# Dividing the filling down unit of a seven-product pair into two halves by blocks of tokens

## The chip, the core and the metric

One core of one Trainium2 chip runs the whole program, in one launch. The metric is the time of that launch on the device in microseconds (us), the median of three runs; smaller is better.

## The reference, cut to what matters

Ten stages follow each other on a matrix x of 256 tokens by 1024 features, in fp32. Six of them are feed-forward blocks and are all that the change touches:

```
def swiglu(h, w_gate, w_up, w_down):
    return (jax.nn.silu(h @ w_gate) * (h @ w_up)) @ w_down
```

Two of these have 2816 hidden features (22 tiles of 128), four have 4096 (32 tiles; gate and up are then the two halves of one matrix). The other four stages (two mixers of the first model, two hybrid mixers of the second) hold attention, retention and a delta rule.

## The kernel before, in words

**Split operands.** Every fp32 weight is split into two parts of type fp32r: `hi`, a rounded copy, and `lo`, the rest (`prep`, L139). A product of two split matrices is three matmuls, hi·hi, hi·lo and lo·hi (`mm3`, L270). A *unit* is one weight block of up to 128 x 2048 numbers. It is loaded in two halves of 128 x 1024 by SyncE's DMA queue (L151), ScalarE (ACT) casts each to `hi` (L154), VectorE (DVE) subtracts to get `lo` (L155). `hi` and `lo` have four buffers each. `pump` (L193) prepares units until four are ready ahead of the last one used (AHEAD), so a unit that has been used up gives its buffer to the one four places later.

**A feed-forward block** (`ffn`, L614) goes over chunks of 256 hidden features, C = 11 or 16 of them. An ordinary chunk (`chunk`, L653) multiplies x by a gate unit and an up unit and makes h = silu(gate)·up. Each chunk has also a *down* unit, which multiplies its h by the chunk's rows of w_down and adds into four PSUM accumulators y (`emit_down`, L755): for each block b of 128 tokens 12 matmuls of 512 columns, 24 in all. The down units of a chunk are emitted after the next chunk's gate and up products (`downs`, L771).

**The seven-product pair** (`quad`, L704) takes two chunks at once, c and c+1, at c = 3 and 7 (C = 11) or 3, 7 and 11 (C = 16): 2·2 + 4·3 = 16 pairs in the program. By a scheme in the manner of Strassen's it needs seven products of 128-token blocks where eight would do it plainly; each is 12 matmuls of 512 columns. Their names and order are 11, T1, T2, T3, 21, T4, 22. The weights of T1 to T4 are differences of weight blocks, made by DVE in fp32 before the split (`combine`, L160); the sums of x are made once for each block (`sums`, L677), at its start. Three PSUM banks p, q, r take the products: 11 and 21 go to p, T2, T3 and T4 to q (T3 and T4 are added onto what is there, start=False), T1 and 22 to r.

DVE reads the banks between the products: `add(u2, p1, q)` after T2 (L725; called **the u2 add** here), `add(u3, p1, q)` after T3 (L728; **the u3 add**), `add(u3, u3, r)`, then `add(g1, p1, q)` after T4, and so on; all of these show as line L279 with `s<-s,work`, 128x512. T3 adds into q, so it can't start before the u2 add has read q; T4 likewise waits for the u3 add. Between T2 and T3 stands `fill()` (L726): one open down unit, both blocks, 24 matmuls. Between T3 and T4 stands the product 21, 12 matmuls.

**What sets the order.** TensorE (PE) runs in the order of the program text (`manual_schedule`, L780). The other engines' instructions are put in order when the program is compiled: the tile scheduler goes through the work in time order and takes on each engine, of what is ready, what stands first in the program text. On the chip each engine then runs its own list in that order. The preparation that a product's `pump` asks for stands in the text right behind the product, and so ahead of the addition that reads the product's bank.

Of the kernel before, what the change touches and what calls it, by code (L numbers as in the profile page):

```python
# [98 lines left out]
def kslab(w, k0, k1, c0, c1):  # L99
    return w[128 * k0:128 * k1, c0:c1].reshape(k1 - k0, 128, c1 - c0).transpose(1, 0, 2)  # L100
# [18 lines left out]
class Net:  # L119
# [494 lines left out]
    def ffn(self, nt, gate, up, down, nxt):  # L614
# [4 lines left out]
        hs = {}  # L619
# [33 lines left out]
        def chunk(c):  # L653
            ps = []
            for src in (gate, up):
                def fn(inp, src=src):
                    w, a, z = cols(src, c)(inp)
                    return kslab(w, 0, 8, a, z)
                u = self.unit((8, 256), fn)
                p = self.tile(512)  # L660
                for j in range(2):
                    self.fold(p, j, self.x_tile(u, j))
                    if late and (src is up or j == 1):
                        late.pop(0)()
                ps.append(p)
                if src is gate:
                    sg = self.tile(512)
                    self.act(sg, p, AF.Silu)
                    self.pump()
            h = self.tile(2, 256)  # L670
            self.mul(h.rearrange("p a b -> p (a b)"), sg, ps[1])
            hp = self.pair(2)
            self.split(hp[0], hp[1], h)
            self.pump()
            return hp
# [28 lines left out]
        def quad(c, fill):  # L704

            def cut(src, k, inp):
                return kslab(src[0](inp), 4 * k, 4 * k + 4, src[1] + 256 * c, src[1] + 256 * c + 512)
            data = {"11": (gate, 0), "T1": (up, 0), "T2": (up, 1), "21": (gate, 1)}

            def product(ps, mode, l, start):  # L710
                fn = (lambda inp: cut(*data[mode], inp)) if mode in data else None
                w = self.unit((4, 512), fn, mode)
                for k in range(4):
                    self.mm3(ps, (l[0][:, k], l[1][:, k]), (w[0][:, k], w[1][:, k]), start and k == 0, k == 3, True)
                self.pump()

            def x(b, k):
                return tuple(t[:, 4 * k:4 * k + 4, 128 * b:128 * b + 128] for t in self.xT)
            p, q, r = (self.work() for _ in range(3))
            p1, u2, u3, sg, g1 = (self.tile(512) for _ in range(5))  # L720
            product(p, "11", x(0, 0), True)
            self.cp(p1, p)
            product(r, "T1", S[1], True)
            product(q, "T2", S[2], True)
            self.add(u2, p1, q)  # L725
            fill()  # L726
            product(q, "T3", S[3], False)
            self.add(u3, p1, q)  # L728
            self.add(u3, u3, r)
            product(p, "21", x(0, 1), False)  # L730
            self.act(sg, p, AF.Silu)
            product(q, "T4", x(1, 1), False)
            self.add(g1, p1, q)
            self.act(g1, g1, AF.Silu)
            self.mul(u3, u3, g1)
            product(r, "22", S[4], False)
            self.add(u2, u2, r)
            self.mul(u2, u2, sg)
            hq = {}

            def back(b, h):
                def fn():
                    hq[b] = self.tile(4, 128, dt=F32R), self.tile(4, 128, dt=F32R)
                    ps = self.work()
                    for k in range(4):
                        self.tr(ps[:, 128 * k:128 * k + 128], h[:, 128 * k:128 * k + 128])
                    self.split(hq[b][0], hq[b][1], ps.rearrange("p (k t) -> p k t", k=4))
                return fn
            late.extend([back(1, u3), back(0, u2)])
            return [lambda j, b, i=i: tuple(t[:, 2 * i + j] for t in hq[b]) for i in range(2)]  # L750

        def unit_down(c):
            return self.unit((2, 1024), lambda inp: kslab(down(inp), 2 * c, 2 * c + 2, 0, 1024))

        def emit_down(c, b, w, js=range(2), ns=range(2)):  # L755
            for j in js:
                for n in ns:
                    self.mm3(y[b][n], hs[c](j, b),
                             (w[0][:, j, 512 * n:512 * n + 512], w[1][:, j, 512 * n:512 * n + 512]),
                             c == 0 and j == 0, c == C - 1 and j == 1)  # L760

        def plain(hp):
            return lambda j, b: tuple(t[:, j, 128 * b:128 * b + 128] for t in hp)
# [5 lines left out]
        open_ = list(range(HEAD))  # L769

        def downs(n=1000):  # L771
            while open_ and n:
                n -= 1
                e = open_.pop(0)
                w = unit_down(e)
                for b in range(2):
                    emit_down(e, b, w)
                self.pump()
        c = HEAD
        with self.tc.manual_schedule(engines={mybir.EngineType.PE}):  # L780
            while c < C:
                if c in QUADS[C]:
                    hs[c], hs[c + 1] = quad(c, lambda: downs(1))
                    new = [c, c + 1]
                else:
                    hs[c] = plain(chunk(c))
                    new = [c]
                c += len(new)
                if c == C - 1:
                    self.load_next(nxt)  # L790
                downs()
                open_ += [e for e in new if e < C - TAIL]
# [1018 lines left out]
```

## Time and profile before

| | |
|---|---|
| median of 3 runs | 2328.01 us (2327.23 to 2329.88) |
| the profiled execution's own time | 2330.61 us |
| its span | 2328.5 us |
| PE busy | 2279.9 us (98%) |
| DVE busy | 1817.3 us (78%) |
| ACT busy | 1312.9 us (56%) |
| moved by DMA | 419.08 MB, mean 180 GB/s |

The profiled execution's own time is its span and some 2.1 us around it. Times in rows are microseconds from the start of the span. Matmuls overlap: one of 512 columns shows a length of 0.39 us but the next starts 0.23 us later, so lengths of waits are read from starts.

### The profile page before, as it was taken

The page shows a single profiled execution, that of the slowest core. Times are in us where ns is not written, and L with a number is a line of the kernel's source. Part 1 is how long each engine was busy: PE and PEld are TensorE (multiplying, and loading weights), DVE is VectorE, ACT ScalarE, POOL GpSimd, SP SyncE. Part 2 cuts the span into 40 slices and gives each one's busy share as a digit, 9 for nine tenths or more (in the row PEclk, how much of TensorE's full clock was granted, in tenths as well). Part 3 has the DMA queues.
Part 4 walks back from the last instruction along what each step waited for, and adds up shares of the span by engine and source line. Part 5 has one row for each costly group of instructions (what it writes and reads, how often), then busy time and mean ns, then how long its engine had stood idle before and what let it go on. Part 6 is the DMA issues. An engine that isn't in the chain of part 4 may idle for free.

```text
span 2328.5 us, 31780 instructions
## 1 busy us (share of the span) xinstructions
PE 2279.9 (98%) x12094; PEld 1946.6 (84%) x12094; DVE 1817.3 (78%) x2424; ACT 1312.9 (56%) x1950; POOL 93.9 (4%) x149
## 2 busy tenths in 40 slices
PE   8999999999999999999999999999999999999998
PEld 7788888887887888878998888878888889988887
DVE  6688776679859886887678888698877876778885
ACT  6655554455646555764555556465556654555663
POOL 4200000000000000000000000000000000000000
PEclk9999999999999999999999999999999999999999
DMA  7365555565366535543265663565555533576532
GB/s 242 132 226 186 188 197 173 191 237 200 125 229 210 190 132 204 179 156 123 91 213 213 217 217 136 192 227 187 167 178 197 172 105 101 174 259 208 204 130 91
DMA packets 120552, 419.08 MB, mean 180 GB/s; under 512 B 14408, under 2 KB 17224, under 8 KB 120400
## 3 DMA queue, kind: packets, MB, share of 16 engines
q1 hardware_dynamic: 120112, 416.53, 52.7%
q8 instruction: 95, 1.56, 0.3%
q10 hardware_dynamic: 288, 0.52, 0.1%
q14 instruction: 57, 0.47, 0.1%
HBM read 415.95 MB, written 1.05 MB: 179 GB/s over the span
## 4 chain that ended last, share of the span: by engine, by line
PE 45%; DVE 6%; DMA 2%; issue 1%; POOL 1%; ACT 0%; SPq 0%; POOLq 0%; DVEq 0%; ACTq 0%
PE acc L268 24%; PE work L268 20%; DVE lo L155 3%; DVE s L279 2%; PE work L276 2%; DMA raw<-in_w 1%; DMA s<-in_w 1%; POOL c L311 0%; ACT hi L154 0%; SPq L166 0%; POOL c L312 0%; DVE s L291 0%; DVE c L1460 0%; DVE x L279 0%; DVE s L552 0%
## 5 line engine op out<-in xcount | busy, mean ns | idle before, releaser
L155 DVE TENSOR_TENSOR lo<-raw,hi 128x1024 fp32r<-128x1024 f32 (+3 forms) x644 | 755.0, 1204 | 196.0 <-ACT hi L154 186.4
L154 ACT CAST hi<-raw 128x1024 fp32r<-128x1024 f32 (+3 forms) x644 | 642.3, 1035 | 311.3 <-PE work L268 87.5
L268 PE MATMUL acc<-hi,s 128*128 128x512 f32 (+1 forms) x1736 | 550.3, 391 | 0.0
L268 PEld LDWEIGHTS acc<-hi,s 128*128 128x128 f32 x1736 | 325.9, 188 | 66.3 <-ACT s L301 0.6
L268 PE MATMUL work<-x,hi 128*128 128x512 f32 x1472 | 371.8, 394 | 5.9 <-DVE s L279 5.9
L268 PE MATMUL work<-hi,x 128*128 128x512 f32 x1024 | 328.8, 392 | 10.9 <-DVE s L279 10.3
L268 PE MATMUL acc<-lo,s 128*128 128x512 f32 (+1 forms) x868 | 338.0, 389 | 0.0
L279 DVE TENSOR_TENSOR s<-s,s 128x512 f32<-128x512 f32 (+3 forms) x378 | 310.9, 849 | 31.9 <-ACT s L301 21.6
L154 ACT CAST hi<-s 128x1024 fp32r<-128x1024 f32 x224 | 228.9, 1051 | 166.8 <-DVE s L279 72.1
L268 PEld LDWEIGHTS work<-x,hi 128*128 128x128 f32 x1472 | 266.7, 188 | 57.7 <-DVE s L279 8.0
L155 DVE TENSOR_TENSOR lo<-s,hi 128x1024 fp32r<-128x1024 f32 x224 | 266.0, 1219 | 50.1 <-ACT hi L154 48.8
L268 PEld LDWEIGHTS work<-hi,x 128*128 128x128 f32 x1024 | 191.9, 188 | 54.0 <-ACT hi L154 12.6
L268 PEld LDWEIGHTS work<-x,lo 128*128 128x128 f32 x1472 | 200.7, 190 | 14.5
L268 PE MATMUL acc<-x,hi 128*128 128x512 f32 x800 | 207.9, 402 | 0.0
L268 PE MATMUL work<-x,lo 128*128 128x256 f32 x1472 | 205.2, 282 | 0.0
L268 PE MATMUL work<-lo,x 128*128 128x512 f32 x512 | 200.0, 391 | 0.0
L268 PEld LDWEIGHTS acc<-lo,s 128*128 128x128 f32 x868 | 163.3, 188 | 31.5 <-issue 0.2
L268 PEld LDWEIGHTS acc<-x,hi 128*128 128x128 f32 x800 | 145.7, 191 | 28.0 <-issue 1.0
L268 PE MATMUL work<-hi,s 128*128 128x512 f32 x512 | 165.9, 390 | 1.4 <-DVE s L279 1.4
L279 DVE TENSOR_TENSOR s<-work,s 128x256 f32<-128x256 f32 (+4 forms) x286 | 131.4, 471 | 36.5 <-ACT s L301 24.1
L301 ACT COPY s<-work 128x256 f32<-128x256 f32 (+3 forms) x268 | 113.2, 431 | 81.8 <-PE work L268 54.3
L268 PE MATMUL work<-s,s 128*128 128x128 f32 (+8 forms) x884 | 125.0, 300 | 8.0 <-ACT s L301 7.3
(115 smaller groups left out, 2249.4 us busy)
## 6 DMA issues: line engine op xcount, KB each, us to landing
raw<-in_w SPq DMA_DIRECT2D x620, 512.0 KB, 4.9
s<-in_w SPq DMA_DIRECT2D x128, 512.0 KB, 6.6
s<-in_rows SPq DMA_DIRECT2D x16, 512.0 KB, 5.7
raw<-in_w SPq DMA_DIRECT2D x12, 288.0 KB, 3.2
s<-in_rows SPq DMA_DIRECT2D x9, 256.0 KB, 5.3
raw<-in_w SPq DMA_DIRECT2D x4, 384.0 KB, 7.8
raw<-in_w SPq DMA_DIRECT2D x4, 256.0 KB, 4.4
s<-in_relb SPq DMA_DIRECT2D x2, 512.0 KB, 4.1
```

Of the source, the lines that this page charges most:

```text
L154: self.nc.scalar.copy(hi[:, a:b], raw)
L155: self.nc.vector.tensor_tensor(out=lo[:, a:b], in0=raw, in1=hi[:, a:b].bitcast(F32), op=ALU.subtract)
L268: self.nc.tensor.matmul(out, lhsT=l, rhs=r, start=start, stop=stop, skip_group_check=more)
L276: self.nc.tensor.transpose(out, src, self.ident)
L279: self.nc.vector.tensor_tensor(out=out, in0=a, in1=b, op=op)
L301: self.nc.scalar.copy(out, a)
```

## The change

The filling of a pair is cut in two. `fill` becomes a function of the block: `fill(0)` takes the open down unit and emits its 12 matmuls for the first 128 tokens where the whole filling stood, ahead of T3; `fill(1)` emits the 12 for the other 128 tokens between 21 and T4, and calls `pump`. The unit keeps its buffers from one to the other. No instruction is added or taken away on any engine, and the units are used in the same order.

```diff
             product(q, "T2", S[2], True)
             self.add(u2, p1, q)
-            fill()
+            fill(0)
             product(q, "T3", S[3], False)
             self.add(u3, p1, q)
             self.add(u3, u3, r)
             product(p, "21", x(0, 1), False)
             self.act(sg, p, AF.Silu)
+            fill(1)
             product(q, "T4", x(1, 1), False)
...
+        half = {}
+
+        def fill(b):
+
+            if b == 0:
+                half["e"] = open_.pop(0)
+                half["w"] = unit_down(half["e"])
+            emit_down(half["e"], b, half["w"])
+            if b == 1:
+                self.pump()
         c = HEAD
...
-                    hs[c], hs[c + 1] = quad(c, lambda: downs(1))
+                    hs[c], hs[c + 1] = quad(c, fill)
```

## Rows read from the trace of the kernel before

**Rows 1.** The page, part 1: busy us, share of the span, instructions by engine

```profile
PE 2279.9 (98%) x12094; PEld 1946.6 (84%) x12094; DVE 1817.3 (78%) x2424; ACT 1312.9 (56%) x1950; POOL 93.9 (4%) x149
```

**Rows 2.** Waits of PE: line, for whom, us in total, times, longest us

```profile
PE work L268 <- DVE s L279: 17.5, 21, 1.7
```

**Rows 3.** Timeline of PE, first pair (start us, us, what, idle before and releaser)

```profile
169.63 0.39 PE L268 MATMUL acc<-hi,s 128*128 128x512 f32 x1
...
174.84 0.39 PE L268 MATMUL acc<-hi,s 128*128 128x512 f32 x1
175.45 0.47 PE L268 MATMUL work<-hi,s 128*128 128x512 f32 x1 [0.21 <-DVE s L279]
...
178.25 0.39 PE L268 MATMUL work<-hi,x 128*128 128x512 f32 x1
...
182.86 0.47 PE L268 MATMUL work<-hi,x 128*128 128x512 f32 x1 [1.73 <-DVE s L279]
```

**Rows 4.** Timeline of DVE in the same pair

```profile
172.35 2.35 DVE L279 TENSOR_TENSOR s<-s,s 128x1024 f32<-128x1024 f32 x2
174.62 0.68 DVE L279 TENSOR_TENSOR s<-s,work 128x512 f32<-128x512 f32 x1
175.22 4.62 DVE L155 TENSOR_TENSOR lo<-s,hi 128x1024 fp32r<-128x1024 f32 x4
179.76 2.35 DVE L155 TENSOR_TENSOR lo<-raw,hi 128x1024 fp32r<-128x1024 f32 x2
182.03 0.68 DVE L279 TENSOR_TENSOR s<-s,work 128x512 f32<-128x512 f32 x1
```

**Rows 5.** Timeline of PE, second pair: down, T3

```profile
236.13 0.39 PE L268 MATMUL acc<-hi,s 128*128 128x512 f32 x1
...
241.57 0.39 PE L268 MATMUL work<-hi,s 128*128 128x512 f32 x1
```

**Rows 6.** Timeline of DVE in the second pair

```profile
232.26 4.85 DVE L155 TENSOR_TENSOR lo<-s,hi 128x1024 fp32r<-128x1024 f32 x4
237.02 1.22 DVE L279 TENSOR_TENSOR s<-s,s 128x1024 f32<-128x1024 f32 x1
238.16 1.22 DVE L155 TENSOR_TENSOR lo<-s,hi 128x1024 fp32r<-128x1024 f32 x1
239.29 0.68 DVE L279 TENSOR_TENSOR s<-s,work 128x512 f32<-128x512 f32 x1
...
242.91 2.36 DVE L155 TENSOR_TENSOR lo<-s,hi 128x1024 fp32r<-128x1024 f32 x2 [1.80 <-ACT hi L154]
```

**Rows 7.** Timeline of the sixth block, first and last pair: down, u2 add

```profile
2111.94 0.39 PE L268 MATMUL acc<-hi,s 128*128 128x512 f32 x1
...
2116.93 0.68 DVE L279 TENSOR_TENSOR s<-s,work 128x512 f32<-128x512 f32 x1
...
2242.48 0.39 PE L268 MATMUL acc<-hi,s 128*128 128x512 f32 x1
...
2245.65 0.68 DVE L279 TENSOR_TENSOR s<-s,work 128x512 f32<-128x512 f32 x1
```

**Rows 8.** Stretches (after POOL: granted clock, DMA share, GB/s); timeline of PE

```profile
74.70:81.50 6.80, 5.14 (x13) 4.12 (x14) 5.48 (x17) 4.73 (x8) 1.86 (x3) 0.50 0.25 80
180.50:184.00 3.50, 1.77 (x8) 1.19 (x7) 3.50 (x5) 2.49 (x3) 0.00 (x0) 1.00 0.98 342
...
75.69 1.22 PE L268 MATMUL work<-s,s 128*128 128x128 f32 x4 [2.89 <-ACT s L301]
...
1026.68 0.87 PE L268 MATMUL work<-s,s 128*64 128x256 f32 x4 [2.21 <-ACT s L301]
...
1017.91 2.00 PE L268 MATMUL acc<-x,hi 128*128 128x512 f32 x8
...
1033.60 3.76 PE L268 MATMUL acc<-x,hi 128*128 128x512 f32 x8
```

**Rows 9.** Timeline of PE: the longest wait behind a second pair

```profile
1645.59 1.65 PE L268 MATMUL work<-x,hi 128*128 128x512 f32 x6 [1.47 <-DVE s L279]
```

## The prediction

> **What bounds the kernel now.** I read the page first: PE is busy for 98% of the span, DVE for 78% [rows 1]. No work is added or removed, so the change can only move PE's waits. The view of waits comes next: in the work banks PE waits for DVE's L279 for 17.5 us in 21 waits, none over 1.7 us [rows 2]. So all that better filling could win is some 0.8% of the time, and what counts is where these waits stand. For that I read the timelines of PE and DVE in every pair and find two kinds.
>
> *Kind A*, the first pair of each block, six of them. DVE is behind, for it has made the sums of x just before. The down matmuls run from 169.63 to 174.84, one each 0.227 us (23 steps in 5.21 us), so their slot ends at 175.07; T3 starts at 175.45, a wait of 0.38 us. T3 and 21 follow, T4 should start at 180.97 and does at 182.86, a wait of 1.89 us [rows 3]. DVE says why: the u2 add, wanted from the end of T2 at 169.63, comes at 174.62 behind the subtractions of T4's weights and ends at 175.30; the u3 add, wanted from 178.25, comes at 182.03 behind six splits, the last two of them of a unit that T3 has just let in [rows 4].
>
> *Kind B*, the other ten. PE waits nowhere. T2 ends at 236.13, the filling covers 5.44 us, T3 starts at 241.57 [rows 5]. But here too the u2 add stands behind a row of splits without a pause and ends only at 239.97, 3.84 us after T2 [rows 6]. Nobody sees this today, because the filling is longer than 3.84 us. The last pair of each kind repeats it: 2117.61 − 2111.94 = 5.67 us in A, 2246.33 − 2242.48 = 3.85 us in B [rows 7]; the pairs between lie within 0.03 us of these.
>
> **The change part by part.**
>
> *The filling ahead of T3 is halved*: 12 matmuls by 0.227 = 2.72 us of cover where 5.44 stood. The u2 add doesn't come earlier for it. All that stands ahead of it on DVE belongs to units whose place in the text, and whose buffers, the change leaves alone; up to T3 the order is made from the same facts. T3 starts 0.15 us after the add's end (175.30 to 175.45) [rows 3, 4].
> - Kind B: the half filling ends at 236.13 + 2.72 = 238.85, T3 can start at 239.97 + 0.15 = 240.12: a new wait of 1.27 us [rows 5, 6]. Ten of them: +12.7 us. The bounds are nothing (if the order on DVE moved) and 1.27; the rows are this very place, so I take the upper one.
> - Kind A: T3 starts when it did, the wait grows from 0.38 to 3.10 us.
>
> *The other half moves ahead of T4.* Kind A: T4 can start at 175.45 + 2.80 (T3, from 175.45 to 178.25) + 2.72 (21) + 2.72 (half) = 183.69, against 182.86 before [rows 3]. The u3 add must be done by then. Before, it had six splits ahead of it; after, 22's buffer comes free only with T3's end, not with the filling's, so DVE has only T4's two splits left, and those end at some 177.5, half of the four that start at 175.22 [rows 4]. The u3 add should then run at T3's end and be done near 179. T4's wait of 1.89 us is gone, T3's has grown by 2.72: +0.83 us a pair, six of them: +5.0 us. In kind B there was no wait at T4 to win back.
>
> *The down unit keeps its buffer longer.* The next `pump` is T3's; it asks for two units where one buffer is free. Counted in matmuls each later unit still gets its buffer where it did: 22's unit at T3's end, which stands where the filling's end stood, the next at 21's end, which stands where T3's did. In B, 22's splits ended at 242.91 + 2.36 = 245.27, 3.70 us after the buffer came free; from T3's new end at 242.84 that is 246.54, and 22 starts at 251.0 [rows 5, 6]. Cost nothing; cover 4.5 us, and without it 22 would wait for the rest. The loads on SP's queue are the same, in the same order; what their issue waits for moves along with PE. POOL has no part in it. Also priced at nothing: `fill(1)`'s pump, which finds nothing to prepare.
>
> *The longer wait and PE's clock.* This has no row in a pair, so I bound it. Up to 1.89 us, no wait in a pair cost clock: 180.5 to 184 was granted 1.00. An idle stretch of 2.89 us, up to 75.69, had a fall to 0.50 in it, from 2.4 to 1.2 GHz, that lasted the 6.8 us from 74.7. Behind one of 2.21 us, up to 1026.68, eight matmuls of 512 columns take 3.76 us where they had taken 2.00 shortly before, 0.22 us more each; and this stretch has a twin in the other hybrid block [rows 8]. At the lower level 6.8 us hold about 16 such matmuls, so a fall costs up to 16·0.2 = 3.2 us. Kind A's new wait of 3.10 us is longer than all of these. Bounds: 0 and 6·3.2 = 19.2 us. Behind two of the three came sparse small products, while here dense ones follow, and some of the low stretch will lie in the wait itself. So I take a fall in four of six, at half the price: 4·1.6 = +6.4 us.
>
> *Given back later?* Three second pairs have a wait some 9 us behind them, 1.47 us the longest [rows 9]; a PE that is 1.27 us later could meet its data there. At most 1.5 us for that one, and less for the others; I take nothing and keep it for the lower end.
>
> Sum: 12.7 + 5.0 + 6.4 = +24.1 us. The profiled execution took 2330.6 us, 2.6 above the median of the runs shown; on it the sum gives 2354.7, on the median 2328.0 + 24.1 = **2352.1 us**. A run can tell a change of about 0.2%, or 4.7 us.
>
> **The rivals.**
>
> *Faster: the u2 add moves up.* If the scheduler put it right at T2's end, it would be done 0.7 us later and half a filling would do. All waits of kind A's would go: 6·(0.38 + 1.89) = 13.6 us, to 2314.4. It decides at the place of one instruction in DVE's list. For it: the list is made anew, and each pair's wait shifts what follows. Against it: 16 pairs of 16 show the same two places, in blocks of two lengths, with the add behind work that stands ahead of it in the text. 0.08. If it moves in some pairs only, or half of the way, sums near zero come out: 0.04.
>
> *The u3 add stays late.* If the splits of the unit that follows 22 keep ahead of it, they now wait for 21's end, 180.97 instead of 178.25. The add ended 4.46 us after that event (182.71), so it would end at 185.43, T4 start at 185.58 instead of 183.69: 6·1.89 = 11.3 us more, 2363.4. Against it: DVE runs dry at T3's end, so the add finds no rival there. 0.06.
>
> *Every long wait costs the clock.* Six falls at full price: 12.7 + 5.0 + 19.2 = 36.9, to 2364.9. For it: three of three. Against it: the dense matmuls behind. 0.10. The Trainium skill, "TensorE: Matmul & The Clock Gate", section "HAM oscillation — how this bites in real kernels", says that a matmul stream broken by waits can have its clock throttled again at each of them, so that each next group starts at half rate; by that rule this rival is the sum. The 1.89 us waits of the trace disagree, its longer ones agree.
>
> That the change is undone when the list is made can't be: PE's order is the text's.
>
> **How the numbers follow.** The forecast, with none to most of the falls, has 0.72: without a fall and with 2.4 us given back it ends at 2328.0 + 17.7 − 2.4 = 2343.3. The range takes in the two slower rivals at the top and a small loss of kind B's waits at the bottom: 2340 to 2366, with the faster rival and the sums near zero left out (0.12). Faster 0.08, same 0.04, slower 0.72 + 0.06 + 0.10 = 0.88.
>
> **What would show it.** In the changed kernel's timeline, each of the ten pairs of kind B should have T3 start some 4.0 us after T2's end with an idle of about 1.1 to 1.3 us released by DVE's L279; each of the six of kind A a T3 wait of about 3 us, and no wait ahead of T4. In the view of waits L268 <- L279 should rise from 17.5 to about 35 us, longest near 3. The granted clock should show half-rate stretches just behind the first pairs. If the u2 add ends less than 2.6 us after T2, the forecast is wrong in its main term; if T4 still waits, the u3 add was misjudged; if the clock stays at 1.00, the sum is 17.7.

## The result and the profile after

| | before | after |
|---|---|---|
| median (lowest to highest) | 2327.62 us (2323.51 to 2329.88), 4 runs | 2358.05 us (2354.63 to 2364.09), 4 runs |
| ratio of the two | | 1.0135 [1.0121, 1.015] |
| profiled execution's own time | 2330.61 us | 2354.63 us |
| its span | 2328.5 us | 2352.6 us |

The divided filling makes the kernel slower by 2358.05 − 2327.62 = 30.4 us. The forecast was +24.1 us, to 2352.1, with a range of 2340 to 2366.

The spans differ by 2352.6 − 2328.5 = 24.1 us, which is the forecast's sum to the tenth. That is chance: the profiled execution of before lies 3.0 us above its median, that of after is the fastest of its four and lies 3.4 us below; 24.1 + 3.0 + 3.4 gives 30.5, the difference of the medians but for rounding.

The page's part 1 of the changed kernel shows the same numbers of instructions as [rows 1]; PE's busy time is 6.1 us longer and DVE's 5.2:

```profile
PE 2286.0 (97%) x12094; PEld 1948.5 (83%) x12094; DVE 1822.5 (77%) x2424; ACT 1310.2 (56%) x1950; POOL 93.9 (4%) x149
```

The view of PE's waits, the line that answers to [rows 2] (line, for whom, us in total, times, longest us):

```profile
PE work L268 <- DVE s L279: 35.6, 26, 3.0
```

It rose from 17.5 to 35.6 us, and the longest wait from 1.7 to 3.0. Where these waits stand is seen in the timelines. PE in the changed kernel, first and second pair of the first block, then the first pair of the third block (start us, us, what, idle before and releaser):

```profile
170.57 0.39 PE L268 MATMUL acc<-hi,s 128*128 128x512 f32 x1
...
173.06 0.39 PE L268 MATMUL acc<-hi,s 128*128 128x512 f32 x1
176.40 0.47 PE L268 MATMUL work<-hi,s 128*128 128x512 f32 x1 [2.95 <-DVE s L279]
...
180.82 0.39 PE L268 MATMUL work<-hi,x 128*128 128x512 f32 x1
...
186.06 0.39 PE L268 MATMUL acc<-hi,s 128*128 128x512 f32 x1
186.29 0.39 PE L268 MATMUL work<-hi,x 128*128 128x512 f32 x1
...
191.73 1.07 PE L268 MATMUL work<-x,hi 128*128 128x512 f32 x4
...
239.45 0.39 PE L268 MATMUL acc<-hi,s 128*128 128x512 f32 x1
...
241.94 0.39 PE L268 MATMUL acc<-hi,s 128*128 128x512 f32 x1
243.44 0.47 PE L268 MATMUL work<-hi,s 128*128 128x512 f32 x1 [1.11 <-DVE s L279]
243.75 0.40 PE L268 MATMUL work<-lo,s 128*128 128x512 f32 x1
...
257.17 1.98 PE L268 MATMUL work<-x,hi 128*128 128x512 f32 x8
...
739.51 0.39 PE L268 MATMUL acc<-hi,s 128*128 128x512 f32 x1
...
745.34 0.47 PE L268 MATMUL work<-hi,s 128*128 128x512 f32 x1 [2.94 <-DVE s L279]
...
759.02 1.30 PE L268 MATMUL work<-x,hi 128*128 128x512 f32 x5
```

- Second pair (kind B): the half filling starts at 239.45 and its last matmul at 241.94, so its slot ends at 242.17; T3 starts at 243.44, a wait of 1.27 us where there was none [rows 5]. All ten pairs of the kind have 1.27 or 1.28.
- First pair (kind A): T3 starts 5.83 us after T2's end, as before (5.82, [rows 3]), but waits 3.11 of them. T4 follows the second half at 186.29, 0.23 after that half's last matmul, without a wait. All six have a T3 wait of 3.10 to 3.12 and no wait at T4.
- From T2's end to the chunk behind the pair it is 17.72 us in the second pair, 21.16 in the first, and 19.51 in the pair at 739.51.

The timeline of PE before gives the starts of the chunks behind the first two pairs, to compare with:

```profile
188.40 0.61 PE L268 MATMUL work<-x,hi 128*128 128x512 f32 x2
...
252.45 0.62 PE L268 MATMUL work<-x,hi 128*128 128x512 f32 x2
```

From T2's end that was 188.40 − 169.63 = 18.77 and 252.45 − 236.13 = 16.32 us.

DVE in the changed kernel, first and second pair, shows why T3 waits:

```profile
173.29 2.37 DVE L279 TENSOR_TENSOR s<-s,s 128x1024 f32<-128x1024 f32 x2
175.56 0.70 DVE L279 TENSOR_TENSOR s<-s,work 128x512 f32<-128x512 f32 x1
...
181.02 1.41 DVE L279 TENSOR_TENSOR s<-s,work 128x512 f32<-128x512 f32 x2 [2.49 <-PE work L268]
...
240.34 1.22 DVE L279 TENSOR_TENSOR s<-s,s 128x1024 f32<-128x1024 f32 x1
241.48 1.22 DVE L155 TENSOR_TENSOR lo<-s,hi 128x1024 fp32r<-128x1024 f32 x1
242.62 0.68 DVE L279 TENSOR_TENSOR s<-s,work 128x512 f32<-128x512 f32 x1
```

The list has not moved: the u2 add stands behind the same subtraction and split as in [rows 6] and ends at 243.30, 3.85 us after T2 (3.84 before). In the first pair it ends at 176.26, 5.69 after T2, again as before. The u3 add at 181.02 found DVE idle for 2.49 us and ran the moment T3 was done.

The windows view of the changed kernel shows the price of the long wait (us, busy us of PE, PEld, DVE, ACT, POOL, granted clock, DMA share, GB/s):

```profile
174.00:176.80 2.80, 0.40 (x2) 0.39 (x3) 2.80 (x4) 2.09 (x2) 0.00 (x0) 1.00 0.79 262
176.90:180.20 3.30, 3.30 (x9) 2.51 (x9) 1.63 (x2) 0.00 (x0) 0.00 (x0) 0.50 0.79 241
180.30:190.00 9.70, 9.70 (x44) 7.98 (x44) 8.43 (x9) 7.30 (x8) 0.00 (x0) 1.00 0.78 269
745.30:755.00 9.70, 9.66 (x43) 8.05 (x44) 8.30 (x9) 6.09 (x8) 0.00 (x0) 1.00 0.84 277
1038.00:1048.00 10.00, 8.89 (x49) 6.68 (x50) 7.76 (x19) 4.47 (x17) 0.48 (x1) 1.00 0.48 158
```

Just behind the wait of 3.11 us, T3 runs at 0.50, from 2.4 down to 1.2 GHz, until 180.2; then the clock is 1.00 again. Such a stretch of 3.4 us stands behind five of the six long waits; behind the one up to 745.34 there is none. That pair is 1.65 us shorter (19.51 against 21.16): a fall costs 1.65 us.

The last of these rows is the first hybrid stage at full rate. Before, the same stage held a half-rate stretch, as the windows view of before shows:

```profile
1030.00:1037.00 7.00, 7.00 (x25) 6.09 (x25) 5.81 (x15) 3.05 (x13) 0.00 (x0) 0.50 0.39 119
```

The change doesn't touch this stage, and another profiled execution of the changed kernel (below, run again) has such a stretch there too; it is one of the things that differ between executions of one kernel. Here it favours the changed kernel.

The pairs of the two traces add up so, each from T2's end to the chunk behind it:

| term | forecast | measured |
|---|---|---|
| kind B, ten pairs | 10·1.27 = 12.7 | 13.8 (17.68 to 17.72 against 16.32) |
| kind A without the clock, six | 6·0.83 = 5.0 | 4.3 (19.51 against 18.80 on average: 0.71) |
| clock | 4·1.6 = 6.4 | 5·1.65 = 8.2 |
| sum | 24.1 | 26.3 |

Outside the pairs the two profiles differ too, and the same timelines give by how much. The two stretches that hold the hybrid stages (from the chunk behind the seventh pair to T2's end in the eighth, and from behind the thirteenth to the fourteenth) took 410.0 and 408.2 us before, 405.6 and 407.7 in the changed kernel: 4.9 us less. All else outside the pairs is 2.6 us longer. With the distances of the two profiles from their medians, 26.3 + 2.6 − 4.9 + 3.0 + 3.4 = 30.4 us, the measured difference.

### The profile page after: what moved, and what is told of

The parts are those of the page before. It is cut to its first block, busy times and chain, and to the rows that moved or that the text cites. A ratio compares the mean times of both kernels' runs of the same rounds, so it can differ in the third digit from the quotient of the medians.

```text
span 2352.6 us, 31811 instructions
## 1 busy us (share of the span) xinstructions
PE 2286.0 (97%) x12094; PEld 1948.5 (83%) x12094; DVE 1822.5 (77%) x2424; ACT 1310.2 (56%) x1950; POOL 93.9 (4%) x149
## 4 chain that ended last, share of the span: by engine, by line
PE 80%; DVE 12%; DMA 3%; issue 2%; ACT 1%; POOL 1%; SPq 0%; DVEq 0%; POOLq 0%; ACTq 0%
PE work L268 40%; PE acc L268 37%; DVE lo L155 6%; DVE s L279 5%; PE work L276 3%; DMA raw<-in_w 2%; ACT hi L154 1%; DMA s<-in_w 1%; POOL c L311 0%; POOL c L312 0%; SPq L166 0%; DVE s L291 0%; POOL c L998 0%; POOL c L997 0%; DVE x L279 0%
## 5 line engine op out<-in xcount | busy, mean ns | idle before, releaser
L279 DVE TENSOR_TENSOR s<-s,s 128x512 f32<-128x512 f32 (+3 forms) x378 | 311.8, 853 | 32.4 <-ACT s L301 21.6
L268 PE MATMUL work<-hi,s 128*128 128x512 f32 x512 | 172.3, 403 | 28.8 <-DVE s L279 28.8
L268 PEld LDWEIGHTS work<-hi,s 128*128 128x128 f32 x512 | 99.2, 194 | 55.9 <-ACT hi L154 35.1
```

The costliest lines, as they stand in the source:

```text
L268: self.nc.tensor.matmul(out, lhsT=l, rhs=r, start=start, stop=stop, skip_group_check=more)
L279: self.nc.vector.tensor_tensor(out=out, in0=a, in1=b, op=op)
```

## The experiments

**Theory.** The cost is the place of the u2 add in DVE's list. DVE takes it behind weight preparation that stands ahead of it in the text, and the halved filling no longer covers that. **Rivals:** that dividing the unit is what costs (its buffer kept longer, loads later), or that the clock makes most of the loss.

### Additions ahead of the preparation, filling divided

From the changed kernel, the additions behind T2 and T3 are moved in the text ahead of the preparation that the product's `pump` asks for. The arithmetic is the same.

```diff
-            def product(ps, mode, l, start):
+            def product(ps, mode, l, start, then=None):
...
+                if then:
+                    then()
                 self.pump()
...
-            product(q, "T2", S[2], True)
-            self.add(u2, p1, q)
+            product(q, "T2", S[2], True, lambda: self.add(u2, p1, q))
             fill(0)
-            product(q, "T3", S[3], False)
-            self.add(u3, p1, q)
-            self.add(u3, u3, r)
+            def third():
+                self.add(u3, p1, q)
+                self.add(u3, u3, r)
+            product(q, "T3", S[3], False, third)
```

> The changed kernel, but the u2 add and the two u3 adds stand in the text ahead of the preparation that T2's and T3's pump asks for, so that DVE's list has them earlier; the filling stays divided. If the new waits come from the place of the u2 add in DVE's list: in kind B it should end some 1.7 us after T2 instead of 3.85 and T3 should not wait; in kind A it should end near 3.4 us, T3 wait about 0.8 us instead of 3.1; no half-rate stretch at the pairs; about 2319 us (before, 2328, less 13.6 for the old waits, plus 6 x 0.8). If instead the waits come from the down unit holding its buffer or from weights that come late, they stay: T3 waits of 1.27 and 3.1 us, near 2358 us.

Measured: 2330.01 us (2323.28 to 2334.39, 10 runs), before beside it 2327.85 (25 runs): 1.0009 [0.9994, 1.0023]. DVE's timeline in the second pair, then PE's:

```profile
237.98 0.68 DVE L279 TENSOR_TENSOR s<-s,work 128x512 f32<-128x512 f32 x1
238.58 1.22 DVE L155 TENSOR_TENSOR lo<-s,hi 128x1024 fp32r<-128x1024 f32 x1
239.71 1.22 DVE L279 TENSOR_TENSOR s<-s,s 128x1024 f32<-128x1024 f32 x1
```

```profile
239.57 0.39 PE L268 MATMUL acc<-hi,s 128*128 128x512 f32 x1
239.80 0.39 PE L268 MATMUL work<-hi,s 128*128 128x512 f32 x1
```

The u2 add now comes ahead of the split and the subtraction and ends 1.58 us after T2's end at 237.08. T3 follows the half filling without a wait, in all ten pairs of kind B; in kind A the add ends 3.42 after T2, T3 waits 0.83 to 0.85, and no pair has a half-rate stretch. The unit is divided as in the changed kernel, and some 28 of the 30 us are gone: nearly all of the loss was the add's place, not the division. The expected time of 2319 us was not reached, though. Inside the pairs all is as forecast; the rest came back behind them. In its trace some 7 us of waits stand in the chunks behind pairs, 1.42 the longest, where before had 2.5. Its median also lies 4 us above the profiled execution's 2325.86; that part is open.

### Additions ahead of the preparation, filling whole

The same moves on the kernel before.

```diff
-            product(q, "T2", S[2], True)
-            self.add(u2, p1, q)
+            product(q, "T2", S[2], True, lambda: self.add(u2, p1, q))
             fill()
...
+            product(q, "T3", S[3], False, third)
```

> The kernel before (filling whole, ahead of T3) with the same three additions moved ahead of the preparation in the text. By the theory of the place in DVE's list kind A's wait at T3 (0.38 us) goes and the one at T4 (1.89 us) shrinks to about 0.1; kind B stays without waits: about 2315 us, and dividing the filling is then worth nothing or costs 4 us (against e1). If the old waits had another cause, 2328 us.

Measured: 2328.6 us (2323.0 to 2333.07, 10 runs), 1.0001 [0.9988, 1.0014]: a miss. The waits of kind A are gone (T3 none, T4 0.24 us), and the chunk starts 16.7 us after T2 instead of 18.8. But the view of PE's waits has a new line:

```profile
PE work L276 <- DVE s L279: 9.7, 8, 2.4
PE work L268 <- DVE s L279: 4.4, 9, 1.2
```

L276 are transposes of the pair's result u3, which the chunk behind does between its own products. The timelines of PE, DVE and ACT in that chunk of the second block:

```profile
572.07 0.66 PE L276 MATMUL work<-ident,s 128*128 128x128 f32 x4 [1.63 <-DVE s L279]
...
566.87 0.68 DVE L279 TENSOR_TENSOR s<-s,work 128x512 f32<-128x512 f32 x1
569.05 2.36 DVE L155 TENSOR_TENSOR lo<-raw,hi 128x1024 fp32r<-128x1024 f32 x2 [1.50 <-ACT hi L154]
571.33 0.68 DVE L279 TENSOR_TENSOR s<-s,s 128x512 f32<-128x512 f32 x1
...
567.97 2.18 ACT L154 CAST hi<-raw 128x1024 fp32r<-128x1024 f32 x2 [2.28 <-DMA raw<-in_w]
570.06 0.62 ACT L298 ACTIVATE s<-s 128x512 f32<-128x512 f32 x1
```

The same fault one product later. The addition behind T4 (566.87) is followed by silu on ACT, which stands behind two casts; these wait 2.28 us for a load. Then comes the product u3·g1 on DVE at 571.33, behind the splits of the same units, and only then can PE transpose, at 572.07. In the kernel before, DVE's timeline has u3·g1 at 567.36, 19.7 us after T2 (at 547.70), and PE came to the transposes only at 24.4; the casts ahead of that silu waited for no load there. Here it is 23.3 us after T2 (571.33 against 548.06), and PE, which came to the chunk 2.1 us earlier, wins only 0.4 of it at the transposes (24.0). Of 12.8 us won up to the chunk's start (six times 2.1), 3.7 are left at the transposes.

### Filler in the long wait

The changed kernel with 12 matmuls of 512 columns into a bank that nobody reads, between the half filling and T3 of each first pair. They are extra work: 72 matmuls.

```diff
             fill(0)
+            if c == 3:
+                spare = self.work()
+                flat = S[1][0].rearrange("p k t -> p (k t)")
+                for k in range(12):
+                    self.mm(spare, self.xT[0][:, k % 8, 0:128], flat)
```

> The changed kernel with 12 matmuls of 512 columns into a spare PSUM bank, read by nobody, between the first half of the filling and T3 of the first pair of each block (72 matmuls more in all). They take 2.72 us of the 3.10 us that PE waits there, so T3 should start when it did. If the half-rate stretches there are part of the price, the granted clock stays at 1.00 at all six places and the time falls by 5 or 6 times 1.6 us, to about 2349 us, with more work. If the clock is no part of the price, the time stays near 2358 us; if the spare matmuls are not hidden, it rises by up to 16 us to 2374.

Measured: 2352.01 us (2351.34 to 2358.57, 4 runs), 1.0114 [1.0084, 1.0144]. PE's timeline at the first pair:

```profile
172.60 2.88 PE L268 MATMUL work<-s,x 128*128 128x512 f32 x12
175.72 0.47 PE L268 MATMUL work<-hi,s 128*128 128x512 f32 x1 [0.23 <-DVE s L279]
...
189.44 1.98 PE L268 MATMUL work<-x,hi 128*128 128x512 f32 x8
```

The windows view of the same place (columns as above, the granted clock third from the end):

```profile
174.00:186.00 12.00, 11.77 (x52) 9.46 (x51) 10.56 (x11) 8.36 (x9) 0.00 (x0) 1.00 0.87 280
```

T3 starts when it did, 5.83 us after T2's end at 169.88, but the clock is 1.00 at all six places. The chunk behind the pair starts 19.56 us after T2's end, as in the pair without a fall (19.51) and not as in those with one (21.16); the other five have 19.51 to 19.56. So the low stretch and its price go when the wait is filled. The median is some 6 us below the changed kernel's (2358.05 to 2352.01), about what four falls cost at 1.65 us each, but the two were not run side by side and the intervals of their ratios overlap (1.0114 [1.0084, 1.0144] and 1.0135 [1.0121, 1.015]): the gain in time is not shown by the medians alone. By the pairs, the clock makes a fifth (four falls, 6.6 us) to a good quarter (five, 8.2) of the 30 us, not most of it.

### Eighteen matmuls ahead of T3, six ahead of T4

The changed kernel with the unit cut at three quarters: 18·0.227 = 4.09 us of filling would cover the 3.85 us that T3 needs in kind B, with DVE's list as it is.

```diff
-            emit_down(half["e"], b, half["w"])
-            if b == 1:
+            if b == 0:
+                emit_down(half["e"], 0, half["w"])
+                emit_down(half["e"], 1, half["w"], (0,))
+            else:
+                emit_down(half["e"], 1, half["w"], (1,))
                 self.pump()
```

> The changed kernel with the filling divided 18 to 6 matmuls: the first block and half of the second ahead of T3, the rest ahead of T4. 18 matmuls cover 4.08 us. By the theory kind B needs 4.00 us, so its wait goes; kind A waits 1.75 us at T3 with the clock at 1.00, and T4 starts 5.83 + 2.80 + 2.72 + 1.36 = 12.71 us after T2, 0.5 earlier than before: about 2328 - 3 = 2325 us. If dividing the unit costs by itself (the unit held longer), it stays near 2350 us or above.

Measured: 2335.82 us (2332.22 to 2341.85, 10 runs), 1.0034 [1.0022, 1.0047]. Inside the pairs it is as expected: no wait in kind B, 1.73 to 1.75 us at T3 in kind A, no half-rate stretch in any pair. The time is a miss, again from behind the pairs. PE, DVE and ACT in the chunk behind the second pair:

```profile
261.84 1.45 PE L268 MATMUL work<-x,hi 128*128 128x512 f32 x5 [1.07 <-DVE s L279]
...
258.23 1.23 DVE L155 TENSOR_TENSOR lo<-raw,hi 128x1024 fp32r<-128x1024 f32 x1 [2.50 <-ACT hi L154]
261.11 0.68 DVE L279 TENSOR_TENSOR s<-s,work 128x512 f32<-128x512 f32 x1
...
257.14 1.05 ACT L154 CAST hi<-raw 128x1024 fp32r<-128x1024 f32 x1 [3.39 <-DMA raw<-in_w]
```

The expected time was 2325 us. The addition behind 22 is done at 261.79, 24.4 us after T2 (at 237.35) and 8.1 after 22, whose end is the chunk's start 16.34 after T2. It stands behind the split of a load that came late. Such waits, mostly of 0.7 to 1.2 us, stand behind most of the second and third pairs and come to 9.5 us in this trace.

### First pairs alone, other pairs alone, and the change again

Three kernels side by side: the division only where c is 3 (the first pair of each block), only where it isn't, and in all.

```diff
             fill(0)
+            if not c == 3:
+                fill(1)
...
-            fill(1)
+            if c == 3:
+                fill(1)
             product(q, "T4", x(1, 1), False)
```

(The second kernel has `c != 3` in both places.)

> The filling is divided in the first pair of each block alone (six pairs, kind A); the other ten have it whole ahead of T3. If the terms stand side by side, this costs 6 x 0.75 us of waits and five or six half-rate stretches of 1.6 us: about 2328 + 13 = 2341 us, with T3 waits of 3.1 us and the clock at 0.50 behind most of them. If the clock is no part of the price, 2332 us.

> The filling is divided in the ten pairs of kind B alone. By the theory each loses 1.37 us (the wait of 1.27 and a slower first matmul behind it): 2328 + 13.7 = 2341.5 us, no half-rate stretch at any pair. If a wait in kind B were given back by loads that come in meanwhile, it stays below 2335 us.

> The changed kernel as it is, once more, beside the two that each do one half of it. If the two halves add up, its distance from the kernel before is the sum of theirs: about 27 us, 2355 us; the first result, four runs, gave 30. The half-rate stretches should come at four to six of the first pairs in each execution, not always at the same ones, and not at the ten others.

| kernel | median, 4 runs each | ratio to 2325.24 us (7 runs) | over it |
|---|---|---|---|
| first pairs alone | 2341.88 us | 1.0067 [1.0052, 1.0082] | 16.6 |
| other pairs alone | 2344.68 us | 1.0079 [1.0064, 1.0094] | 19.4 |
| all | 2357.62 us | 1.0138 [1.0123, 1.0153] | 32.4 |

The parts are real and add up within their intervals (36.0 against 32.4, each known to some 3.5 us). The waits in the pairs are those of the first trace: 3.10 to 3.12 in the first pairs with three falls of the clock, 1.27 in the others with none. But each kernel costs more than its pairs show: 9.0 and 13.7 us by the timelines of the first two, 24.6 in the third. Of that third kernel's other 7.8 us the traces place most. Outside the pairs and the two hybrid stretches it is 6.6 us longer than the profile of before (the first two 3.0 and 4.5): waits behind its pairs come to 4.4 us where before had 2.5, and those ahead of its first pairs to 5.1 where before had 3.8. In the hybrid stretches it is 4.5 us shorter, and the profile of before, 2330.61 us, lies 5.4 above this round's median of 2325.24. With 0.4 us by which the third kernel's own profile lies below its median, 24.6 + 6.6 − 4.5 + 5.4 + 0.4 is the 32.4 but for rounding. So what the forecast lacked stands mostly in the ordinary stretches around the pairs, as waits that grow.

### The last two additions first, in the changed kernel

Is it the work behind T4 and 22 that makes this remainder? In the changed kernel only that is moved ahead of the preparation.

```diff
-            product(q, "T4", x(1, 1), False)
-            self.add(g1, p1, q)
-            self.act(g1, g1, AF.Silu)
-            self.mul(u3, u3, g1)
-            product(r, "22", S[4], False)
-            self.add(u2, u2, r)
-            self.mul(u2, u2, sg)
+            def fourth():
+                self.add(g1, p1, q)
+                self.act(g1, g1, AF.Silu)
+                self.mul(u3, u3, g1)
+            def last():
+                self.add(u2, u2, r)
+                self.mul(u2, u2, sg)
+            product(q, "T4", x(1, 1), False, fourth)
+            product(r, "22", S[4], False, last)
```

> The changed kernel with only the additions behind T4 and 22 ahead of the preparation; the u2 and u3 adds stay where they were. The waits at T3 (1.27 and 3.1 us) should stay and the half-rate stretches with them. What goes are waits some 6 us behind the pairs, where an addition stands behind splits of weights that load late: if those are the rest of the measured 30 us over the 24 forecast, the time falls by 3 to 6 us, to about 2353 us; if not, it stays at 2357.

Measured: 2356.74 us (2354.62 to 2357.99, 4 runs), 1.0116 [1.01, 1.0132]. The pairs are unchanged (1.28 and 3.10 to 3.12 us, four falls). The interval overlaps that of the change itself (1.0138 [1.0123, 1.0153]), so the time doesn't tell them apart. The trace shows what became of the waits behind the pairs: where the changed kernel, run again, has them some 7 us behind the chunk's start (idle 4.1 us in all, 0.77 the longest), here they stand some 10 us behind it (5.2 us, 1.26 the longest). They moved and did not go. Why they grow in the first place stays open.

### All additions first: filling whole, 12 and 12, 18 and 6

If the second and fourth kernel lost their gain to the work behind T4 and 22, moving that work as well should show it. Both moves together (T2 and T3 as in the first experiment, T4 and 22 as in the last), with the three ways to fill.

> The filling whole as before, and every addition and product on the banks (behind T2, T3, T4 and 22) ahead of the preparation in the text. With three of them moved, the pairs lost their waits but the time stayed at 2328: the waits came back some 6 us behind the first pairs, where the loads are late. If those are late additions that stand behind splits of late loads, they go too, and the time falls to about 2322 us. If the loads themselves set the pace there, PE waits for the next weights instead and the time stays at 2327 to 2329.

> The changed kernel (12 and 12 matmuls) with all additions and products on the banks ahead of the preparation in the text. If the place in DVE's list is all that made the division dear, it costs next to nothing now: kind B no wait, kind A about 0.85 us at T3 instead of 0.25 at T4, so 6 x 0.6 = 4 us more than with the filling whole: about 2318 us against 2314.7. If dividing costs by itself, 2330 us or more.

> All additions first, filling divided 18 to 6. 18 matmuls cover 4.08 us, kind A's addition needs 3.55: no wait at T3, and T4 has 6 more matmuls of cover against its 0.25 us: every wait inside the pairs gone, about 2313 us, 1 us less than the whole filling. The down unit holds its buffers for six matmuls longer than in the whole filling; if that delays the loads behind it, 2316 us or more.

| kernel | median | ratio to before |
|---|---|---|
| filling whole | 2314.66 us (4 runs) | 0.9952 [0.9936, 0.9969] |
| 12 and 12 | 2323.2 us (10 runs) | 0.998 [0.9968, 0.9992] |
| 18 and 6 | 2313.53 us (4 runs) | 0.9933 [0.9913, 0.9954] |

The view of PE's waits with the filling whole:

```profile
PE work L268 <- DVE s L279: 5.3, 6, 1.3
PE work L276 <- DVE s L279: 0.7, 1, 0.7
```

DVE's timeline of the same kernel in the chunk where the second experiment had its wait:

```profile
564.84 0.69 DVE L279 TENSOR_TENSOR s<-s,s 128x512 f32<-128x512 f32 x1
565.45 1.22 DVE L155 TENSOR_TENSOR lo<-raw,hi 128x1024 fp32r<-128x1024 f32 x1
```

The transposes' 9.7 us are down to 0.7. u3·g1 runs at 564.84, 17.9 us after T2 (at 546.92), where it ran 23.3 after in the second kernel (571.33 against 548.06); the loads are still late (a cast waits 1.36 us at 568.22) but nothing of the pair stands behind them. So the miss of the second kernel, and that of the fourth, was the list and not the loads. This version beats both the kernel before, by 10.6 us, and the changed one; it is also better than the 2322 us expected of it. (Each ratio in the table is to the kernel before as it ran beside that kernel: 2325.24 us for the first, 2328.45 for the other two.)

With the list in order, dividing the unit is harmless only if enough of it stays ahead of T3. At 12 and 12, T3 of the first pairs still waits 0.83 to 0.85 us: DVE still has splits to finish there, and the add ends 3.42 us after T2 against 2.72 of filling. But 2323.2 us is a miss against the 2318 expected. The pairs cost 3.6 us more than with the filling whole; the other 5 us or so lie outside them: behind its pairs this trace has 5.4 us of idle, 1.70 the longest, and that of the whole filling 0.6. PE's and DVE's timelines at the longest:

```profile
1645.18 1.65 PE L268 MATMUL work<-x,hi 128*128 128x512 f32 x6 [1.70 <-DVE s L279]
...
1642.44 2.35 DVE L155 TENSOR_TENSOR lo<-raw,hi 128x1024 fp32r<-128x1024 f32 x2
1644.71 1.02 DVE L279 TENSOR_TENSOR s<-work,s 128x256 f32<-128x256 f32 x2
```

Here it is the ordinary chunk's own read of a bank that stands behind two splits. Whether the loads behind these splits are later because the divided unit keeps its buffer longer was not tested, so a cost of the division of up to some 5 us is not ruled out at 12 and 12. At 18 and 6 there is no wait in any pair, and 2313.53 us is what was expected (2313); its ratio and that of the whole filling overlap, so which of the two is better stays open.

## Why the prediction was right, and where it was not

- **"The u2 add doesn't come earlier for it": right.** It ends 3.85 us after T2 in kind B and 5.69 in kind A, as before. The rival in which it moves up by itself fell; moved up in the text, together with the u3 additions, it takes some 28 us of the change's loss away.
- **Kind B: the wait right, its cost 8% too small.** Forecast 1.27 us, measured 1.27 or 1.28 in ten of ten, but 1.38 at the chunk. Most of the rest is the first matmul behind a wait: the next starts 0.31 us after it (243.44 to 243.75), not 0.23. In all 13.8 instead of 12.7.
- **Kind A: right.** T3 waits 3.10 to 3.12 (forecast 3.10), T4 not at all, 0.71 us a pair instead of 0.83. The u3 add ran at T3's end, so the rival that it stays late fell.
- **The clock: the kind of loss right, its price right partly by luck.** Falls at 1.65 us, forecast 1.6; five of six places here, forecast four. Over the four traces with waits of 3.1 us at the first pairs it was 16 of 24 places, four in six. The forecast halved its bound of 3.2 us because some of the low stretch would lie in the wait itself. That is not what happened: at the first pair it lies wholly behind the wait, under the matmuls, and it is half as long as the 6.8 us that the bound was worked out from (3.4). The rival "every long wait costs the clock full" fell by this price, and by the eight places without a fall. The Trainium skill, "TensorE: Matmul & The Clock Gate", section "HAM oscillation — how this bites in real kernels", tells of a kernel whose clock fell again behind every one of its waits for data; here it happened at two thirds of the waits of 3.1 us and at none of those of 1.27 to 1.89 us in a pair.
- **"Given back later? … I take nothing": the step that came out short.** Measured is 30.4 us (32.4 when run again) against 24.1. Of the 6.3 us, the terms above hold 2.2 (26.3 against 24.1). About 4 us lie outside the pairs. Nothing is given back behind them: the stretches outside the pairs and the hybrid stages are 2.6 us longer in the profiled execution and 6.6 when run again, and waits behind the pairs grow from 2.5 to 3.0 and 4.4 us. The other 1.5 us of the 4 is what differs from execution to execution (−4.9 + 3.0 + 3.4). Executions of the unchanged kernel alone spread from 2321.7 to 2331.6 us in 25 runs; the six of these with a mean granted clock of 0.994 took 2329.5 us on average, the three with 0.997 took 2322.9. The execution that the rows were read from had 0.994, with 10.2 and 6.8 us at half rate in the two hybrid stretches, which the change doesn't touch.
- **"All that better filling could win is some 0.8%"**, from the 17.5 us of PE's waits: the two best kernels are 0.5% and 0.7% faster, of the size that this bound allows. They got there by DVE's and ACT's lists; the filling alone won nothing.

## What to carry to other kernels

Before taking cover away from an engine, look up when the consumer that it covers really ends, not when its inputs are ready: here the addition was ready at T2's end, needed 0.7 us and came 3.85 us later, in the shadow of a filling of 5.44. Where a scheduler breaks ties by the order of the text, put the reader of a result ahead of the preparation of later work, for all steps of the group at once: moving those behind the first two products gained nothing, since the work behind the third then stood behind a late load, and moving all four gained 0.5%. And price a long wait on TensorE at more than its length where a trace shows the clock falling behind it.

## What the runs showed of the hardware that was not expected

- The same wait of 3.10 to 3.12 us at the same place lowers the clock in one execution and not in another: 16 of 24 places fell to half rate for 3.4 us, eight stayed at 1.00.
- Extra matmuls in a wait can keep the clock up: with 72 of them in those six waits it stayed at 1.00, and the pairs were as short as one without a fall (19.51 to 19.56 us, against 21.16). The median was some 6 us lower, which the intervals of the ratios leave unproven.
- How long a hybrid stage runs at half rate differs from execution to execution, and the time with it: over the thirteen traces the two hybrid stretches had 0 to 10.2 us at half rate each, and took 404.9 to 405.8 us with none and 409.1 to 410.9 with 10.2.
- The first matmul behind a wait takes the next one 0.31 us to follow instead of 0.23, which adds 0.08 us to the cost of each wait.
